# A hybrid attention layer: the attention gate's projection as seven half-size products, and the gated linear attention in steps of two chunks

## The chip, the core and the metric

The kernel runs on one core of a Trainium2 chip. The metric is the device time of one execution in microseconds (us), as the median of several. A core has TensorE (PE, matrix products; its weight loads are PEld), VectorE (DVE), ScalarE (ACT) and GpSimd (POOL), and SyncE (SP), which here issues every DMA. Matrix results go to PSUM, in banks of 512 float32 columns; everything else is in SBUF or in DRAM.

## What is computed

A layer on 1024 tokens (`x`) and 256 context tokens, width 1024. Both are normalised and modulated, and one projection `w_in` gives all streams:

```python
p = h @ w_in          # gq gk gv gg(gate) g_lr | dq dk dv dg(gate) | m_gla m_diff
...
s_f = gla_final_state(kc, vc, la_fc)          # from the context, per direction
o_gla = bidir_gla(q, k, v, la_f, la_b, s_f, s_b)
...
a = merge_heads(rms_norm(o_gla) * gla_gain) * jax.nn.silu(gla_gate)
b = merge_heads(rms_norm(o_diff) * diff_gain * (1 - lam_init)) * jax.nn.silu(diff_gate)
y = jax.nn.sigmoid(m_gla) * (a @ w_br_gla) + jax.nn.sigmoid(m_diff) * (b @ w_br_diff)
return y @ w_out
```

GLA (gated linear attention) has 4 heads with keys of 128 and values of 256 columns. It goes over the tokens in chunks; inside a chunk there are scores `q exp(cum) . k exp(-cum)` under a triangle, and between chunks a state of 128 x 256 that decays and takes in `k^T v`, once forward and once backward. Differential attention has 8 heads, two softmaxes each, with queries and keys normalised and rotated. Its gate `diff_gate` is `dg`, 1024 columns for the 1024 tokens.

## The kernel before

**Precision.** A projection is done in a fast float32 form: each operand is split into a high and a low part, and a product is three matmuls (`mm3`: high-high, high-low, low-high). A split is one ACT copy and one DVE subtraction (`split`). GLA's own products are plain float32, which the profile shows as two records a matmul.

**The order of the work is planned.** The kernel is written as generator tasks, and `Driver` runs them against a small model of engine costs when the program is built; so the order of instructions on PE, ACT, DVE and POOL is fixed by the tasks' priorities (a lower number goes first) and by what that model takes to be ready. `acq(tag)` and `rel(tag)` take and give back buffers of a kind (`TAGS` has the counts); a task that finds none waits. Every operation is issued from one of a few lines: matmuls at L335 (`mm`), transposes at L361 (`tr`), the vector engines at L197 (`emit`), DMAs at L300 (`dma`). So the profile's groups are told apart by their tiles.

**The stages.**
1. `prologue` (to about 110 us): constants, modulation, normalisation, the transposed activations `h`.
2. `stream` in `phase_a` (L857) runs projections as 512-column jobs, one after another at priority 9: `jobs` are gk, gq, and the first half of the GLA gate (`gg[0]`). Beside them `job_lr` and `job_la` make the decays, and `sums` (L886) makes four sums of blocks of `h`, stored as `d_s`. `wstream` loads weights through three `raw` buffers of 512 KB and splits them into `w` (18 tiles: nine blocks).
3. `pairs` (L987) does the value projections `gv` and `dv` by seven products of half-size blocks in place of eight (p1 to p7, with sums of blocks on both sides): two groups `g` of 1024 columns, five row tiles (four of the latent tokens for each half of the rows, one of the context). `pair_weights` (L918) loads the weight blocks and makes their sums. A group's accumulators lie in `mm` (3 banks), `gs`, `go`; the second ones in `tp`, `tp`, `gt`. `copy`, `add`, `out` and `direct` take results out. The blocks of `d_s` come back as `z` in `g5`. With the second group `job_gate` (L745) is started, after all weight blocks are loaded (`ev_pl`): it makes the output gate's vector from `w_ada` on DVE, through `raw`, and stores it as `d_gb`.
4. `to_gla` (L1142) waits for the decays, for `d_gb` and for the pairs' buffers, and starts four `gla_head`s. The late projections go on beside them: `dk[0], gg[1], dk[1], dg[0], dq[0], m, dq[1], dg[1]`; `dg` is a plain job of eight tiles for each 512 columns, with `post_gate` (L1340: tanh on ACT, a product on DVE, a product with `gdif` on POOL, store `d_dg`).
5. When GLA (`ev_b2`) and the late projections (`ev_stream`) are both done, attention starts (`to_b`), with the rest of the projections (`fill`) as filler; then the output (`phase_c`).

**A GLA head** (L1358), 10 chunks of 128 tokens, two of them context; a group `g` is two chunks. `prep` loads keys and decays and scans them on DVE; odd heads use the space `hk` of the context's `h`, which comes free when the last context tile of `dk[1]` is done. `kstates(e)` (L1431), per direction and group: exponential on ACT, product with k on POOL, two transposes, copy to `gkt`, before it goes on to the next group. `backward` runs through the chunks from the last and keeps the states `gsb`; each update (`upd`, L1469) is one matmul into `gt` and one DVE operation. `intra` (L1540), per group: the query factors `gqe` of both directions (ACT, POOL), the score factors (`factors`, L1504: differences, exponentials, products into `gkk` and `gqr`; a POOL memset makes the zero block), then for each chunk eight records of score matmuls into `gs`, a copy, two triangles on POOL (`affine_select`), a sum on DVE (`gsc`); only then the next group. `forward` (L1603), per chunk: three matmuls into `go` (forward state, backward state, scores), then `post` (L1639: square, root, product with the gate's rows, two transposes, split, store `d_aT`), then the forward update.

Of the kernel before, what the change touches and what calls it, by code (L numbers as in the profile page):

```python
# [11 lines left out]
F32R = mybir.dt.float32r  # L12
# [216 lines left out]
class Hybrid:  # L229
# [10 lines left out]
        gk=("sbA2", 1), gla=("sbA2", 2), gq=("sbA2", 1), gsb=("sbA2", 8), gsf=("sbA2", 2), ge=("sbA2", 2),  # L240
        gkt0=("sbA2", 2), gkt1=("sbA2", 2), gqe=("sbA2", 4), gqr=("sbA2", 2), gd=("sbA2", 2), gx=("sbA2", 2),
        gkk=("sbA2", 2), gsc=("sbA2", 2), gp=("sbA2", 4), gpl=("sbA2", 2), gv0=("sbA2", 2), gv1=("sbA2", 2),
# [502 lines left out]
    def job_gate(self):  # L745


        yield self.ev_pl
# [63 lines left out]
    def phase_a(self):  # L812
# [8 lines left out]
        self.gla_done, self.gla_free, self.gla_back, self.gla_intra = ([Event() for _ in range(4)] for _ in range(4))  # L821
# [17 lines left out]
        dg = nat(C_DG, (x8, x8), lambda c, i, pm: self.post_gate(1, c, i, pm))  # L839
        jobs = [tra(C_GK, [0, 1, 2], self.post_gk), tra(C_GQ, [0, 1], self.post_gq), gg[0]]  # L840
        late = [dk[0], gg[1], dk[1], dg[0], dq[0], dq[1], dg[1]]
# [11 lines left out]
        wp = self.pair_weights((C_GV, C_DV), wd.loaded[-1], last)  # L853
# [20 lines left out]
        d.spawn(self.consts_late(), At(105.0), prio=2)  # L874
        d.spawn(self.sums(), prio=3)
# [7 lines left out]

    SUMS = ("s2", "s1", "s3", "s4")

# [32 lines left out]
    def pair_weights(self, cols, ev_load, ev_run):  # L918
# [3 lines left out]
        wp = {(g, n, k): Event() for g in range(2) for n in RIGHT for k in range(4)}  # L922
# [4 lines left out]
        ev_l = {(g, n, kk): Event() for g in range(2) for n, kk, _ in LOADS}  # L927
# [13 lines left out]
        def run():  # L941
            yield ev_run
            for g in range(2):
# [43 lines left out]
    def pairs(self, wp):  # L987
# [3 lines left out]
        def loads():  # L991

            for g in range(2):
# [4 lines left out]
            for g in range(2):  # L998
                for n in self.SUMS:
                    for k in range(4):  # L1000
                        yield self.ev_s[n, k]
                        yield from self.acq("g5")
                        z = self.t("g5", [P, 2, 640], F32R)
                        self.dma(z, self.d_s[n, k])
# [16 lines left out]
        def mms(g, n, k, t, pm, first, last):  # L1021
# [5 lines left out]
            if t == 4:  # L1027
# [6 lines left out]
        for g in range(2):  # L1034
            if g:
                d.spawn(self.job_gate(), prio=2)
# [4 lines left out]
            def out(g, r, c, t, x, tag):  # L1041

                o = self.tok(8 + r if t == 4 else 4 * r + t)
                if g == 0:
# [41 lines left out]
            for t in range(5):  # L1086
# [7 lines left out]
            for n, ev, dst, nxt, tag in (("p6", "x", U, "u", "x2"), ("p5", "u", U5, "u5", "p")):  # L1094
                for k in range(4):
                    for t in range(5):
# [5 lines left out]
            for t in (0, 1, -1, 2, -2, 3, -3, 4, -4, -5):  # L1102
# [9 lines left out]
            for k in range(4):  # L1112
                for t in range(5):
# [6 lines left out]
    def direct(self, g, t, pm, tag):  # L1120

        o = self.tok(8 if t == 4 else t)
        if g == 0:
# [18 lines left out]
    def to_gla(self):  # L1142
# [8 lines left out]
        self.pool.memset(self.fresh.rearrange("p (c t) -> p c t", t=P + 1)[:, :, 0], 0.0)  # L1151
        for h in range(4):
            self.gla_head(h)
# [1269 lines left out]
```

## Time and profile before

| what | us |
|---|---|
| time, median of 3 runs | 1690.53 (1687.66 to 1690.86) |
| the profiled execution's own time | 1693.12 |
| its span, from the first to the last instruction | 1691.4 |
| TensorE busy | 1649.2 |
| VectorE busy | 1140.7 |
| ScalarE busy | 781.4 |
| GpSimd busy | 617.6 |
| pairs, about | 209 to 399 |
| GLA, from the store of `d_gb` to the last store of `d_aT` | 422 to 827 |
| first score matmul of attention | 910.6 |

Times inside a profile count from the span's start. In a row of the profile `mm<-w,h` means that an instruction writes tile `mm` and reads `w` and `h`; `x12` is the number of instructions; "idle before" and "releaser" say how long the engine stood and what it waited for. A matmul's own duration contains the pipeline behind it, so the price of one in a row of them is the distance from start to start.

### The profile page before, as it was taken

Reading aid. Unit: us, or ns where it says so; the run is one execution under the profiler, and the core shown is the slowest. Engines: PE = TensorE matmul, PEld = TensorE weight load, DVE = VectorE, ACT = ScalarE, POOL = GpSimd, SP = SyncE. Lnnn points to the kernel's source line nnn. Section 1 sums busy time; section 2 is a strip of 40 time slices with the busy share of each in tenths; the row PEclk is TensorE's granted clock in tenths of the full one; section 3 lists DMA queues with packets and bytes.
Section 4 is the critical chain, followed back from the end, with each engine's and each line's share of the span. In section 5 each row is a group of like instructions: output and inputs, shape, how many; then the busy total and the mean of one; then the engine's idle time right before and its main releaser. Section 6 shows DMA issues by size and latency. Waiting matters only on the chain.

```text
span 1691.4 us, 24621 instructions
## 1 busy us (share of the span) xinstructions
PE 1649.2 (98%) x8437; PEld 1366.0 (81%) x8437; DVE 1140.7 (67%) x2027; ACT 781.4 (46%) x1632; POOL 617.6 (37%) x743
## 2 busy tenths in 40 slices
PE   7999999999999999999999999999999899999999
PEld 3788888888888888888887788888887787887887
DVE  4787743466856866775553988777787787526694
ACT  4766522343444445455232666655656555411231
POOL 1500300002554655553342555455665455700000
PEclk9999999999999999999999999999999999999999
DMA  8556847588737466453851444436368451279431
GB/s 306 172 202 235 303 159 266 178 280 284 224 119 222 134 177 197 131 177 108 245 163 53 106 116 122 129 91 162 104 172 251 140 164 60 91 234 340 151 100 75
DMA packets 259950, 293.43 MB, mean 173 GB/s; under 512 B 21961, under 2 KB 182641, under 8 KB 259825
## 3 DMA queue, kind: packets, MB, share of 16 engines
q1 hardware_dynamic: 259824, 291.85, 55.0%
q8 instruction: 67, 1.10, 0.3%
q14 instruction: 59, 0.48, 0.1%
HBM read 194.27 MB, written 97.52 MB: 173 GB/s over the span
## 4 chain that ended last, share of the span: by engine, by line
PE 82%; DVE 7%; DMA 5%; ACT 2%; issue 2%; POOL 2%; SPq 0%; DVEq 0%; ACTq 0%; POOLq 0%
PE mm L335 33%; PE mc L335 10%; PE mb L335 7%; PE s L335 6%; PE b L335 5%; PE go L335 4%; PE b L361 3%; PE tp L335 3%; PE gt L335 3%; DVE sm L197 3%; PE gs L335 3%; PE tp L361 2%; POOL at L197 2%; DVE e L197 1%; ACT e L197 1%
## 5 line engine op out<-in xcount | busy, mean ns | idle before, releaser
L335 PE MATMUL mm<-w,h 128*128 128x512 f32 x1608 | 401.6, 400 | 0.0
L335 PEld LDWEIGHTS mm<-w,h 128*128 128x128 f32 x1608 | 297.4, 188 | 60.1 <-issue 0.5
L197 DVE TENSOR_REDUCE sm<-s 128x1 f32<-128x1024 f32 (+1 forms) x192 | 194.5, 1038 | 23.9 <-PE s L335 22.0
L335 PE MATMUL mb<-h,wt 128*128 128x512 f32 x744 | 205.1, 408 | 2.5 <-ACT ft L197 2.1
L197 ACT ACTIVATE e<-s,sm 128x1280 f32<-128x1280 f32 x128 | 170.1, 1331 | 69.2 <-DVE sm L197 61.5
L197 POOL TENSOR_TENSOR at<-ac,at 128x512 fp32r<-128x512 f32 x128 | 185.1, 1446 | 10.7
L335 PE MATMUL s<-hk,aq 128*128 128x512 f32 (+1 forms) x768 | 180.7, 369 | 4.1 <-issue 1.5
L197 POOL TENSOR_SCALAR at<-ac 128x512 fp32r<-128x512 f32 x128 | 100.7, 787 | 202.2 <-ACT ac L197 182.6
L335 PEld LDWEIGHTS mb<-h,wt 128*128 128x128 f32 x744 | 131.1, 190 | 25.9 <-ACT ft L197 3.6
L335 PEld LDWEIGHTS s<-hk,aq 128*128 128x128 f32 x768 | 124.3, 193 | 24.9 <-ACT e L197 4.9
L335 PE MATMUL mm<-h,w 128*128 128x512 f32 x576 | 142.4, 398 | 1.4 <-DVE h L197 1.0
L335 PE MATMUL mc<-h,wt 128*128 128x512 f32 x600 | 140.8, 392 | 1.4 <-DVE wt L197 0.5
L197 POOL TENSOR_TENSOR sm<-sm,nhalf 128x1 f32<-128x1 f32 (+2 forms) x110 | 113.8, 1035 | 56.4 <-DVE sm L197 49.6
L335 PEld LDWEIGHTS mc<-h,wt 128*128 128x128 f32 x600 | 111.4, 188 | 26.1 <-DMA h<-d_bT 2.4
L335 PE MATMUL b<-at,vv 128*128 128x256 f32 x960 | 131.9, 287 | 0.5 <-POOL at L197 0.4
L335 PEld LDWEIGHTS b<-at,vv 128*128 128x128 f32 x960 | 124.1, 192 | 5.7 <-POOL at L197 1.2
L335 PEld LDWEIGHTS mm<-h,w 128*128 128x128 f32 x576 | 106.1, 188 | 23.6 <-DVE h L197 1.5
L197 ACT ACTIVATE p<-mm 128x512 f32<-128x512 f32 (+1 forms) x111 | 64.1, 587 | 130.0 <-PE mm L335 112.0
L197 ACT ACTIVATE ac<-b 128x512 f32<-128x512 f32 x120 | 71.3, 601 | 89.6 <-PE b L361 84.4
L197 DVE SCALAR_TENSOR_TENSOR e<-e,sm,e 128x1280 f32<-128x1280 f32 x64 | 108.7, 1699 | 0.6
L197 DVE TENSOR_TENSOR w<-raw,w 128x512 fp32r<-128x512 f32 x120 | 88.0, 751 | 29.1 <-ACT w L197 24.2
L361 PE MATMUL b<-ident,e 128*128 128x128 f32 x598 | 93.3, 277 | 14.2 <-DVE b1k L197 4.8
(282 smaller groups left out, 2697.4 us busy)
## 6 DMA issues: line engine op xcount, KB each, us to landing
raw<-in_w_in SPq DMA_DIRECT2D x66, 512.0 KB, 4.7
g<-d_s SPq DMA_DIRECT2D x32, 640.0 KB, 5.3
aq<-d_qT SPq DMA_DIRECT2D x128, 128.0 KB, 3.1
d_dv<-pl SPq DMA_DIRECT2D x40, 256.0 KB, 5.3
d_kT<-pl SPq DMA_DIRECT2D x40, 256.0 KB, 2.9
gv<-d_v SPq DMA_DIRECT2D x40, 256.0 KB, 3.2
hk<-d_kT SPq DMA_DIRECT2D x32, 320.0 KB, 5.2
vv<-d_dv SPq DMA_DIRECT2D x16, 640.0 KB, 5.9
```

The lines of the kernel that those rows point to most:

```text
L197: self.ins = f(out, *args, **kw).ins
L335: self.ins = self.nc.tensor.matmul(out, lhsT, rhs, start=start, stop=stop, skip_group_check=more).ins
L361: self.nc.tensor.transpose(out, src, self.ident[:n, :n])
```

## The change

It does five things. **(1)** The gate `dg` leaves the late projections and becomes the third group of `pairs`, with four row tiles, as it has no context (`nt = 4`). `out` gains its tanh, product and POOL product; `direct` uses `post_gate`. **(2)** `job_gate` starts at 110 us on the planner's clock, without waiting for `ev_pl`. **(3)** The late projections are `dk[0], dk[1], gg[1], dq[0], dq[1], m`. **(4)** GLA goes in steps of two chunks: two updates' products in one `gt` bank, six outputs in one `go` bank, scores of two chunks in one `gs` bank, four transposes in one `tp` bank, one square, root, copy, triangle and store for two chunks. **(5)** GLA's tasks are taken apart: `kstates` hands the transposes to `turned`; `intra` makes factors only and hands scores to `pairs`; the query factors are a task `inter`; the forward states are a task `fstates`; `forward` has only outputs. `gkk` becomes one tile for each direction, zeroed once, and differences and exponentials are made in place in it.

```diff
-        late = [dk[0], gg[1], dk[1], dg[0], dq[0], dq[1], dg[1]]
+        late = [dk[0], dk[1], gg[1], dq[0], dq[1]]
...
+        d.spawn(self.job_gate(), At(110.0), prio=2)
...
+    BY7 = (("gv", C_GV), ("dv", C_DV), ("dg", C_DG))
...
-        for g in range(2):
-            if g:
-                d.spawn(self.job_gate(), prio=2)
+        for g, (what, _) in enumerate(self.BY7):
+            nt = 4 if what == "dg" else 5
...
+                if self.BY7[g][0] == "dg":
+                    yield from self.acq("p")
+                    th = self.t("p", [P, 512])
+                    yield d.on("ACT", x)
+                    yield On(self.act.activation(th, x, AF.Tanh, scale=0.5), "DVE")
+                    e = self.dve.scalar_tensor_tensor(x, th, 1.0, x, ALU.add, ALU.mult)
+                    self.rel("p", e)
+                    yield e
+                    xv = x.rearrange("p (n w) -> p n w", w=P)
+                    self.pool.tensor_tensor(xv, xv, self.gdif.unsqueeze(1).to_broadcast([P, 4, P]), ALU.mult)
...
-            for t in (0, 1, -1, 2, -2, 3, -3, 4, -4, -5):
+            for t in (0, 1, -1, 2, -2, 3, -3, 4, -4, -5) if nt == 5 else (0, 1, -1, 2, -2, 3, -3, -4):
...
-                yield AtPE(self.pool.tensor_tensor(ex, st["k"][:, sl], ex, ALU.mult))
...
+                en = self.pool.tensor_tensor(ex, st["k"][:, sl], ex, ALU.mult)
+                d.spawn(turned(e, g, ex, kt, v), AtPE(en), prio=2)
...
+        def products(e, g, js):
+
+            kt, v = st[e, g]
+            yield from self.acq("gt")
+            pu = self.t("gt", [P, 2, 256])
+            for j in js:
+                en = self.mm(pu[:, j], kt[:, j], v[:, j], True, True)
+            yield en
+            return pu
...
+            for g in range(1, 5):
                 qr, kr, ev = [None] * 2, [None] * 2, E(2)
                 for e in range(2):
                     d.spawn(factors(e, g, qr, kr, ev[e]), prio=3)
                 for e in range(2):
                     yield ev[e]
...
+                d.spawn(pairs(g, qr, kr), d.whenpe(*qr, *kr), prio=2)
...
+        def forward():
...
+                yield ev_sc[g]
+                yield ev_qe[g]
+                yield ev_sb[2 * g]
+                yield ev_sf[2 * g + 1]
...
+                po = self.t("go", [P, 2, 256])
                 for j in range(2):
                     c = 2 * g + j
+                    self.mm(po[:, j], qe[0][:, j], st["sf", c], True, False)
+                    self.mm(po[:, j], qe[1][:, j], st["sb", c], False, False)
+                    en = self.mm(po[:, j], sc[:, j, 0], v[:, j], False, True)
...
         d.spawn(prep(), prio=1)
         d.spawn(kstates(1), prio=2)
         d.spawn(bwd(), prio=1 if h else 0)
+        d.spawn(fstates(), prio=0)
         d.spawn(forward(), prio=0)
```

More of the change, by code (lines that the diff above doesn't have):

```diff
@@ L942, in run @@
             yield ev_run
-            for g in range(2):
+            for g in range(len(cols)):
                 def blk(n, k):
@@ L997, in loads @@
             yield self.ev_la
-            for g in range(2):
+            for g, (what, _) in enumerate(self.BY7):
+                w = 512 if what == "dg" else 640
                 for n in self.SUMS:
```

318 lines of the change are left out of this document (168 added, 150 removed).

## Prediction

> **What bounds the kernel now.** I read the page's first lines, then the busy times by stage, then the waits of TensorE in the stage that changes, then the chain.
>
> ```profile
> span 1691.4 us, 24621 instructions
> PE 1649.2 (98%) x8437; PEld 1366.0 (81%) x8437; DVE 1140.7 (67%) x2027; ACT 781.4 (46%) x1632; POOL 617.6 (37%) x743
> PE 82%; DVE 7%; DMA 5%; ACT 2%; issue 2%; POOL 2%; SPq 0%; DVEq 0%; ACTq 0%; POOLq 0%
> ```
>
> ```profile
> core 0: us, PE busy (x) PEld busy (x) DVE busy (x) ACT busy (x) POOL busy (x), PEclk, DMA share, GB/s
> 110.00:209.00 99.00, 99.00 (x462) 82.79 (x461) 78.69 (x104) 62.29 (x90) 12.08 (x8) 1.00 0.71 254
> 209.00:399.00 190.00, 189.12 (x833) 155.94 (x832) 94.07 (x145) 63.61 (x109) 1.82 (x2) 1.00 0.66 232
> 422.00:827.00 405.00, 403.56 (x2034) 338.54 (x2033) 273.55 (x536) 190.95 (x536) 212.39 (x346) 1.00 0.58 170
> 827.00:911.00 84.00, 82.50 (x379) 67.91 (x378) 38.05 (x61) 19.88 (x32) 33.09 (x30) 1.00 0.51 146
> ```
>
> TensorE works 98% of the span and carries 82% of the chain. The stages above are, in order: the first projections; the pairs (value columns by seven products); GLA beside the late projections; the late projections alone. TensorE is full in all four, at granted clock 1.00. In GLA's 405 us, DVE is busy 68%, POOL 52%, ACT 47%: none is near its limit on average, and what TensorE lost to waits there and up to 911 is this little:
>
> ```profile
> PE s L335 <- issue: 1.5, 1, 1.5
> PE tp L361 <- DVE gp L197: 0.7, 1, 0.7
> PE gt L361 <- DVE gsf L197: 0.4, 1, 0.4
> PE go L335 <- DVE gsc L197: 0.2, 1, 0.2
> ```
>
> So GLA's latency is hidden now: the projections (priority 9) fill every gap. A GLA that overlaps better has at most 1.3 us of waits (0.7+0.4+0.2) to give back. What counts is **how many TensorE instructions** remain, and whether new waits appear.
>
> **The change, part by part.**
>
> ```profile
> 208.84 2.72 PE tp L335 x12
> ...
> 875.03 34.08 PE mm L335 x150
> 910.60 2.56 PE s L335 x12
> ```
>
> *1. The gate by seven products.* The chain gives the price of a 512-column projection matmul: 12 in 2.72 us among the pairs, 150 in 34.08 us at the end of the late projections (the gate's own second column block), both 0.227 us. Removed: 2 blocks x 8 tiles x 8 k x 3 = 384. Added: 7 products x 4 k x 4 tiles x 3 = 336. So 48 fewer, 48 x 0.227 = **-10.9 us**, on the path, as TensorE is full where they go and where they come. The new group lasts 336 x 0.227 = 76.3 us.
>
> Beside it new work appears: 28 weight splits, 20 sums of weight blocks, 12 additions, 16 gate products on DVE.
>
> ```profile
> L197 DVE TENSOR_TENSOR w<-raw,w x120: 660/685/1711, 24.6 to 863.7; 128x512 fp32r<-128x512 f32 x120
> L197 ACT ACTIVATE p<-mm x111: 384/598/612, 60.8 to 909.2; 128x512 f32<-128x512 f32 x107, 128x256 f32<-128x256 f32 x4
> ```
>
> ```profile
> raw<-in_w_in SPq DMA_DIRECT2D x66, 512.0 KB, 4.7
> g<-d_s SPq DMA_DIRECT2D x32, 640.0 KB, 5.3
> aq<-d_qT SPq DMA_DIRECT2D x128, 128.0 KB, 3.1
> ```
>
> At 0.69 us that is 76 x 0.69 = 52 us of DVE in 76 us: TensorE hides it, as in the two groups before (94 of 190 us). DMA (size and median landing in the rows): 16 sums at 512 of 640 columns (8.4 MB) and ten weight blocks (5.2 MB) in 76 us are 180 GB/s, with 4 MB of stores 233, against 232 measured in the pairs. One margin shrinks. With four tiles instead of five, a product comes back to tile 0 after 9 matmuls (2.04 us) instead of 12 (2.72); in between ACT must copy that tile out (0.60 us) and two semaphores pass. A weight of t2 must be ready every 2.72 us instead of 3.4, through two sums and a split (three times 0.69 plus ACT 0.6). Cost between 0 (five tiles show no wait) and four tiles' copies and late weights, 4 us; I take **+1.5**.
>
> *2. The output gate's vector (job_gate) starts at 110 us instead of inside the pairs.* Its 16 DVE operations leave the pairs, and with them a wait of 0.9 us, behind which the chain shows a `gb` operation ahead of the weight splits.
>
> ```profile
> PE tp L335 <- DVE p L197: 0.9, 1, 0.9
> ...
> 377.27 0.04 DVE gb L197
> ```
>
> That is **-0.9**. They arrive where DVE is 79% busy (78.69 of 99), and its eight 0.5 MB loads take one of the three `raw` buffers at priority 2, ahead of the weight stream's 3.
>
> ```profile
> L197 DVE SCALAR_TENSOR_TENSOR gb<-raw,col,gb x14: 741/752/1417, 350.5 to 414.3; 128x512 f32<-128x512 f32 x14
> ...
> 114.02 1.59 SPq L300 DMA_DIRECT2D raw<-in_w_in  x2
> ...
> 120.58 0.63 ACT L197 ACTIVATE w<-raw 128x512 fp32r<-128x512 f32 x1 [0.23 <-DMA raw<-in_w_in]
> ```
>
> 16 x 0.75 = 12 us bring DVE to 91 of 99. Behind them in DVE's queue stand weight splits and the sums; behind a gate load in the queue of SP stand weight loads. The page of waits has none for TensorE between 110 and 209, but ACT at 120.58 split a weight the moment it landed: no slack at that switch of projections. If the gate takes the buffer freed at 114, the next weight load goes 1.2 us later and shares the DMA; two switches (about 115 and 160) are exposed. Bounds: 0, and 1.2 plus one load's landing, 4.7, about 6 us in all. I take **+2**.
>
> *3. GLA in pairs of chunks, tasks apart.* The same products: 18 state updates, 32 score matmuls, 24 output matmuls and 16 output transposes a head (each full-precision matmul shows as two records). What could change is the cost of breaking into the projections.
>
> ```profile
> 486.04 0.59 PE L335 MATMUL gt<-gv,gkt 128*128 128x256 f32 x2
> 486.28 1.74 PE L335 MATMUL mm<-w,h 128*128 128x512 f32 x6
> 487.86 0.59 PE L335 MATMUL go<-gsf,gqe 128*128 128x256 f32 x2
> 488.29 0.59 PE L335 MATMUL go<-gsb,gqe 128*128 128x256 f32 x2
> ```
>
> A lone update delays the projection by 0.24 us (486.04 to 486.28), and the six projection matmuls after it last 1.58 instead of 1.36: 0.46 in all. Inside a row the step is 0.43. So each of some 80 merges saves 0.03 by this pair, 2.4 us, or nothing. I take **0** (bounds -2.4 and +2.4). The vector engines do the same elements in fewer, longer instructions; the fixed zero block saves 32 POOL memsets. All this is under TensorE's cover.
>
> *4. Order.* GLA opens after three groups, and the late projections are dk, dk, gg1, dq, dq, m. The rotary table for dq is now loaded at dq's own start; its 0.5 MB and two POOL products take some 8 us, against three PSUM buffers of 5.4 us each: **0**, up to 2.
>
> Sum: -10.9 -0.9 +1.5 +2 = **-8.3 us**. Profiled span 1691.4 becomes 1683.1, that execution's 1693.12 becomes 1684.8; against the median 1690.53, which is 2.6 below the profiled execution, **1682.2**.
>
> **Does GLA still fit?** This is what could undo it.
>
> ```profile
> L300 SPq DMA_DIRECT2D d_gb<-gb x1: 333/333/333, 422.2 to 422.2; - x1
> L300 SPq DMA_DIRECT2D d_aT<-gpl x64: 359/386/925, 495.0 to 827.1; - x64
> L335 PE MATMUL mm<-w,hk x96: 387/392/586, 446.5 to 543.5; 128*128 128x512 f32 x96
> 543.19 0.39 ACT L197 ACTIVATE gp<-go 128x256 f32<-128x256 f32 x1 [0.91 <-PE go L335]
> 614.85 0.39 ACT L197 ACTIVATE gp<-go 128x256 f32<-128x256 f32 x1 [3.22 <-PE go L335]
> ...
> 694.55 0.38 ACT L197 ACTIVATE gp<-go 128x256 f32<-128x256 f32 x1
> ...
> 527.23 2.42 PE L335 MATMUL mm<-w,hk 128*128 128x512 f32 x9
> ```
>
> It opened at 422 (after the gate's store) and stored its last rows at 827: 405 us, with the stream's end at 910.6. After, the pairs end at 399+76 = 475, GLA opens near 485, the stream ends near 902: room 417. Even the old pace fits, barely. It gets shorter: between 543 and 615 no output was made, because head 1 needs `hk`, which the context tiles (mm<-w,hk, the last at 543.5) hold until 121 us after opening. With dk second in line these are tiles 9 to 12 of the late stream: 12 x 24 x 0.227 = 65 us after 475; with transposes and GLA's share of TensorE once it runs (an estimate of 30%: the 18 tiles before the context tiles hold 98 us of matmuls and took the 128 from 399 to 527) about 566, 81 us after opening. So GLA lasts about 365 even at the old pace: 50 us to spare. Heads 2 and 3 need gg1, whose first tile comes near 640, before head 2's outputs: before, these came 272 us after opening (the squares of `go` at 694.6), so at about 717, 40 earlier against the opening.
>
> **The rivals.**
>
> *A, slower: GLA becomes the bound.* The overlap makes DVE and POOL meet more often, and POOL slows.
>
> ```profile
> L197 POOL TENSOR_TENSOR ge<-hk,ge x20: 724/740/1696, 560.5 to 795.5; 128x256 f32<-128x256 f32 x20
> L197 POOL TENSOR_TENSOR gqe<-gq,gqe x32: 721/783/1187, 455.3 to 797.2; 128x256 f32<-128x256 f32 x32
> L197 POOL TENSOR_SCALAR_AFFINE_SELECT gsc<-gsc x64: 284/295/837, 467.2 to 809.1; 128x128 f32<-128x128 f32 x64
> L300 SPq DMA_DIRECT2D aq<-d_qT x128: 512/592/1778, 827.6 to 1408.9; - x128
> ```
>
> The same instruction takes up to 1.70 us where its median is 0.74. If all were as slow as the slowest: 40 x 0.96 + 32 x 0.40 + 32 x 0.54 = 68 us, all on GLA's chain: 365 + 68 = 433, 16 past the room. Then the queries' first four loads (4 x 0.59, plus 3.1 to land by the row above) start late, 5.5 more, and nothing else is left for TensorE: +21.5 - 8.3 = +13, **1704**. It decides from 50 us of lengthening. Against it: the medians sit at the minima, and three vector engines have a third of their time free. Chance 0.14. [...]
>
> *B, no change: the early gate and the tight pairs eat the gain.* Two weight switches with only two buffers, each a landing late (2 x 4.7), in place of +2: -10.9 -0.9 +1.5 +9.4 = -0.9, **1689.6**. For it: the missing slack at 120.58. Against it: only the third and fourth load of a switch are exposed. Chance 0.16.
>
> *C, faster still: breaking in costs more than the pair of rows shows.* If each of 80 merges saves a whole 0.22 us (the excess of the six matmuls), -17.6 more: **1664.6**. Against it: the 0.43 step inside a row. Chance 0.06.
>
> *D, it doesn't do what it says.* The overlap shortens GLA and the time doesn't follow, as TensorE is full anyway: that is inside the forecast.
>
> **How the numbers follow.** Forecast 0.64: with all bounds at their best -10.9 -0.9 -2.4 -1.3 = -15.5, 1675; at its worst up to the edge of "same". Differences of 0.2%, 3.4 us, are about what a measurement of this kernel can tell from none: below 1687.1 is faster, above 1693.9 slower. Faster: 0.64 + 0.06 = 0.70; same 0.16; slower 0.14. The range 1675 to 1694 takes in the forecast and B; A and C, 0.20, are left out.
>
> **What would show it.** Right: 7 x 48 matmuls in about 76 us after 399; the first score matmul near 902 instead of 910.6; the last d_aT store well before, at 830 to 870; TensorE's waits up to then under 6 us. Step 2 wrong: waits for `w` or a weight load between 115 and 170. Step 1 wrong: waits for `x2` or `w` between 420 and 435. A: the last d_aT store after 900 and a hole before the first score matmul. C: runs of projection matmuls nearer to 0.227 each beside GLA.

## The result and the profile after

The changed kernel takes 1695.59 us (median of 15 runs, 1692.97 to 1702.45) against 1689.16 of the kernel before (15 runs, 1686.71 to 1693.02): a ratio of 1.0039 with a 95% interval of 1.0031 to 1.0047. It is **slower by 6.4 us**, 0.4%; the forecast was 1682.2, 0.5% faster, in a range from 1675 to 1694. (The 1690.53 of the kernel before that the forecast starts from is the median of the first three of its 15 runs.) A ratio given with its interval is the record's own, not that of the two medians. Figures by stage come from one profiled execution of each kernel.

First the page of the changed kernel: its span, its busy times and the chain by engine.

```profile
span 1696.0 us, 24386 instructions
...
PE 1644.3 (97%) x8389; PEld 1360.1 (80%) x8389; DVE 1169.1 (69%) x2035; ACT 788.9 (47%) x1624; POOL 601.3 (35%) x649
...
PE 42%; DVE 6%; DMA 2%; ACT 2%; issue 2%; POOL 1%; SPq 0%; DVEq 0%; ACTq 0%; POOLq 0%
```

The 48 matmuls are gone (8389 records against 8437). The share of TensorE in the chain cannot be set against the earlier 82%: here the inferred chain accounts for about 55% of the span in all. The busy times by stage say more: the opening, the three groups of pairs, GLA beside the projections, the projections alone.

```profile
core 0: us, PE busy (x) PEld busy (x) DVE busy (x) ACT busy (x) POOL busy (x), PEclk, DMA share, GB/s
110.00:217.00 107.00, 103.56 (x468) 84.24 (x468) 90.35 (x123) 63.20 (x90) 14.75 (x10) 0.98 0.79 274
217.00:484.00 267.00, 265.35 (x1164) 217.59 (x1163) 138.60 (x206) 94.40 (x165) 18.65 (x13) 1.00 0.66 230
487.00:853.00 366.00, 357.50 (x1824) 301.21 (x1823) 277.40 (x515) 174.49 (x483) 204.30 (x263) 0.99 0.58 173
853.00:919.00 66.00, 65.26 (x298) 53.67 (x297) 22.72 (x36) 16.05 (x26) 14.69 (x14) 1.00 0.56 159
```

Two things are new. TensorE stood 3.4 us in the opening (107.00 less 103.56), where it stood not at all, and 8.5 us in GLA's stage (366.00 less 357.50), where it stood 1.4; and in both the granted clock is below 1.00. The other engines are a little fuller in GLA's stage than before, but far from full: DVE 76% (68% before), GpSimd 56% (52%), ScalarE 48% (47%). Three single waits make 8.4 of these 11.9 us. Here is TensorE's own timeline around each, the wait in square brackets:

```profile
196.84 1.82 PE L335 MATMUL tp<-gb,ones 128*128 128x512 f32 x2 [2.51 <-DVE gb L197]
197.67 4.69 PE L335 MATMUL mm<-w,h 128*128 128x512 f32 x12
```

```profile
655.71 0.94 PE L335 MATMUL mm<-w,h 128*128 128x512 f32 x3
660.05 1.12 PE L361 MATMUL tp<-ident,p 128*128 128x128 f32 x4 [3.40 <-POOL p L197]
660.82 1.63 PE L335 MATMUL mm<-w,h 128*128 128x512 f32 x3
```

```profile
817.28 0.94 PE L335 MATMUL mm<-w,h 128*128 128x512 f32 x3
820.73 0.66 PE L361 MATMUL tp<-ident,p 128*128 128x128 f32 x4 [2.50 <-POOL p L197]
```

Each time a small instruction (a matmul with the ones, or four transposes of one tile) stands ahead of projection matmuls in TensorE's queue and waits for a vector engine. The rows show TensorE taking its queue in order: the projections start only after it. How much they could have done meanwhile differs. After 196.84 a long row of them follows without another wait. At 660 DVE splits the next weights from 656.7 to 657.6 and from 658.4 to 659.1, during the wait, so the projections could have filled a part of it. At 820 hardly any: DVE, too, is behind, and splits their weights only after the wait.

```profile
821.14 1.28 DVE L197 TENSOR_TENSOR w<-raw,w 128x512 fp32r<-128x512 f32 x2
821.88 2.50 PE L335 MATMUL mm<-w,h 128*128 128x512 f32 x5 [0.26 <-DVE w L197]
```

And each wait is followed by something else, which the windows of 2 us around the second one show (the column after POOL's is the granted clock):

```profile
656.00:658.00 2.00, 0.66 (x3) 0.19 (x1) 1.98 (x4) 1.11 (x3) 2.00 (x4) 0.99 0.66 153
658.00:660.00 2.00, 0.00 (x0) 0.00 (x0) 1.98 (x3) 0.00 (x0) 2.00 (x2) 0.50 1.22 313
660.00:662.00 2.00, 1.95 (x7) 1.75 (x8) 0.44 (x2) 0.60 (x1) 1.83 (x2) 0.50 0.52 194
662.00:664.00 2.00, 2.00 (x7) 1.54 (x6) 2.00 (x3) 0.00 (x0) 1.93 (x3) 0.50 0.61 177
664.00:666.00 2.00, 2.00 (x9) 1.71 (x8) 0.21 (x1) 0.00 (x0) 0.00 (x0) 0.81 0.31 90
```

After 3.4 us of standing, TensorE runs at half clock until about 665: 2 us times (0.50 + 0.50 + 0.19) = 2.4 us of work lost while it was busy again. So a wait of 3.4 us cost 5.8.

Adding up such windows from one milestone to the next gives a ledger, in which "idle" is the window less TensorE's busy time, "slow clock" is the window times one less the granted clock (a part of it can fall on idle time), and the pairs start with the first second-product matmul:

| stage | before | after | forecast of the step |
|---|---|---|---|
| start of the pairs | 208.7 | 217.2 (+8.5) | +2 |
| pairs, to their last product | 189.0 | 266.8 (+77.8) | +76.3 +1.5 -0.9 = +76.9 |
| from there to the first score matmul | 512.9 | 434.8 (-78.1) | -87.2 |
| of this idle / slow clock | 3.0 / 0.0 | 9.2 / 5.1 | |
| first score matmul | 910.6 | 918.8 | 902 |

After the first score matmul the two executions differ by -3.6 us (1691.4 - 910.6 against 1696.0 - 918.8). That part lasts 773 to 783 us in the profiles of both kernels and of the eighteen below, with nothing there changed in kind, so I read nothing into it. It also means that one profile cannot show a gain of a few us in the whole time; the medians have to.

### The profile page after: what moved, and what is told of

It is laid out like the page before. It is cut to its first block, busy times and chain, and to the rows that moved or that the text cites. A ratio compares the mean times of both kernels' runs of the same rounds, so it can differ in the third digit from the quotient of the medians.

```text
span 1696.0 us, 24386 instructions
## 1 busy us (share of the span) xinstructions
PE 1644.3 (97%) x8389; PEld 1360.1 (80%) x8389; DVE 1169.1 (69%) x2035; ACT 788.9 (47%) x1624; POOL 601.3 (35%) x649
## 4 chain that ended last, share of the span: by engine, by line
PE 42%; DVE 6%; DMA 2%; ACT 2%; issue 2%; POOL 1%; SPq 0%; DVEq 0%; ACTq 0%; POOLq 0%
PE mc L335 10%; PE mm L335 7%; PE mb L335 7%; PE s L335 6%; PE b L335 5%; DVE sm L197 4%; PE b L361 3%; DVE e L197 2%; POOL at L197 1%; ACT e L197 1%; DMA h<-d_bT 1%; PE mz L335 1%; PE go L335 1%; PE tp L361 1%; DMA b1k<-d_dg 0%
## 5 line engine op out<-in xcount | busy, mean ns | idle before, releaser
L335 PE MATMUL mm<-w,h 128*128 128x512 f32 x1260 | 321.4, 404 | 0.9 <-DVE w L197 0.6
L335 PEld LDWEIGHTS mm<-w,h 128*128 128x128 f32 x1260 | 233.3, 190 | 48.9 <-DVE w L197 1.4
L335 PE MATMUL mm<-h,w 128*128 128x512 f32 x576 | 136.7, 394 | 3.1 <-ACT p L197 1.5
L197 POOL TENSOR_TENSOR sm<-sm,nhalf 128x2 f32<-128x2 f32 (+2 forms) x94 | 108.0, 1149 | 53.8 <-DVE sm L197 48.3
L197 ACT ACTIVATE w<-raw 128x512 fp32r<-128x512 f32 x120 | 72.5, 629 | 74.5 <-DVE raw L197 22.8
```

What stands on the lines that cost most here:

```text
L197: self.ins = f(out, *args, **kw).ins
L335: self.ins = self.nc.tensor.matmul(out, lhsT, rhs, start=start, stop=stop, skip_group_check=more).ins
```

## The experiments

**The theory** from these profiles: the instructions were priced rightly, and the loss is these waits of small instructions in TensorE's in-order queue, with the slow clock behind them. The rivals: all of it is the early gate; or GLA's new tasks make the waits; or the plan, drawn anew, would make such waits whatever was changed. ("The early gate" is `job_gate` at 110 us.) Medians are against the kernel before, run beside it on the same chip (1688.7 to 1690.4). The changed kernel was not run again beside them, so differences from its 1695.59 can be off by such 2 us.

### Parts alone

e1 gives the kernel before the early gate only; e2 the third group only (the output gate's vector at its old place, so after the third group's weights); e3 the new GLA only.

```diff
 e1
-        yield self.ev_pl
+        d.spawn(self.job_gate(), At(110.0), prio=2)
...
-            if g:
-                d.spawn(self.job_gate(), prio=2)
 e2   (BY7, nt and the dg branches as in the change; old GLA)
+        late = [dk[0], gg[1], dk[1], dq[0], dq[1]]
+            if g == 1:
+                d.spawn(self.job_gate(), prio=2)
 e3   (the change's gla_head; dg, late and job_gate as before)
```

> The kernel before with one part of the change: the output gate's vector starts at 110 us. Theory (three waits: TensorE's in-order queue holds a small instruction whose operand a vector engine has not finished, at 196, 660 and 820 us of the changed kernel, and TensorE's granted clock is low for some us after each; 3.7, 5.8 and 4.4 us): the wait at the gate's ones matmul comes back, the pairs start 6 to 9 us later than 208.7, the time is 4 to 8 us over the kernel before. Rival (the prediction's step 2: weights late by +2, old wait of 0.9 gone): +1. Rival (all the loss is in GLA's stage): 0.

> The kernel before with one part of the change: the attention gate as a third group of seven products; the old GLA, the output gate's vector with the second group as before, the late projections in the old order without the gate's two jobs. Theory (three waits): 48 matmuls less and no new long wait, -9 us, about 1680. Rival (the shorter late stage leaves GLA's tasks too little cover, so the waits come from it): TensorE waits of 2 us and more before the first score matmul, and less than 4 us gained.

> The changed kernel's GLA (steps of two chunks, tasks apart) alone: two groups of pairs, the attention gate as plain jobs, the old order and the old place of the output gate's vector. Theory (three waits; GLA's tasks fill the queues of ScalarE and GpSimd so that the planned order stands before a tile that is late): one or two waits of 2 us and more at transposes of p between 520 and 850, +5 to +12 us over the kernel before. Rival (the prediction's step 3): within 2 us. Rival (the new order or the third group makes the waits): within 2 us too, and no wait at p.

Measured: e1 1700.69 (1.0062, 1.0046 to 1.0078), e2 1701.53 (1.0066, 1.0049 to 1.0083), e3 1697.64 (1.0041, 1.0027 to 1.0055). Each part alone is slower by 7 to 11 us, 29 in sum, and together they cost 6.4: the parts are not additive. e1 bears the theory out at the start (pairs at 216.6, the wait for `gb` again 2.50) and adds 4.6 us in a GLA stage in which no instruction was changed. e3 loses 7.5 idle and 3.4 slow clock in GLA's stage, in several waits of 1.0 to 1.4, none of them over 2: more than the prediction's 0, but not the one long wait I expected.

e2 was a miss, in an instructive way. TensorE's timeline at the end of its GLA stage:

```profile
914.14 0.41 PE L361 MATMUL tp<-ident,gp 128*128 128x128 f32 x2 [1.65 <-DVE gp L197]
...
917.92 0.41 PE L361 MATMUL tp<-ident,gp 128*128 128x128 f32 x2 [2.08 <-DVE gp L197]
923.46 2.90 PE L335 MATMUL s<-hk,aq 128*128 128x512 f32 x8 [5.12 <-DMA aq<-d_qT]
```

The projections are used up and TensorE waits for GLA's last outputs, then 5.12 us for the first queries. This is the prediction's rival A in its outcome, GLA as the bound, though not by slower vector engines. Its `d_gb` was stored at 521.0 and its last `d_aT` at 919.2: with the gate's vector behind three groups of weights, the old GLA opens late and lasts 398 us.

### The old place of the gate's vector, and the order

e4 is the changed kernel with `job_gate` at its old place; e8 is e2 with the changed kernel's order of the late projections.

```diff
 e4
-        d.spawn(self.job_gate(), At(110.0), prio=2)
+        yield self.ev_pl
+            if g == 1:
+                d.spawn(self.job_gate(), prio=2)
 e8   (e2 with)
+        late = [dk[0], dk[1], gg[1], dq[0], dq[1]]
```

> The changed kernel with the output gate's vector back at its old place (with the second group, after all weight blocks are loaded, here those of three groups). Theory (three waits): the wait at 196 is gone, the pairs start near 209, 6 to 8 us less than the changed kernel, near 1688, and the waits at p in GLA's stage stay. Rival (the prediction's step 2): -1. Rival (the two waits in GLA's stage hang on what came ahead and go too): near 1682.

> As the run of the gate by seven products with the old GLA, but with the changed kernel's order of the late projections (second block of dk second). There GLA ended last: transposes of gp waited at 914 and 918, then the first score matmul 5.1 us for its queries. Theory (the context's space comes free 50 us earlier and GLA fits): last store of d_aT before 895, no such waits, first score matmul near 905, 10 us less than that run. Rival (the old GLA is too slow in any order, so the change's two-chunk GLA is what lets the gate's gain through): waits at gp after 900 again, within 4 us of that run.

Measured: e4 **1684.25** (0.9977, 0.9955 to 0.9998), e8 1699.58 (1.0056, 1.0039 to 1.0073). In e8 the first score matmul waits 5.56 us for its queries again; `d_gb` at 517.6, last `d_aT` at 914.8: 397 us. So the order does not shorten the old GLA when it opens late, and the rival holds: with the late opening, only the two-chunk GLA (e4: 519.0 to 892.1, 373 us) ends before the projections do. Here are e4's opening, its pairs and its GLA.

```profile
110.00:209.00 99.00, 99.00 (x466) 82.94 (x465) 78.74 (x107) 62.55 (x90) 11.18 (x7) 1.00 0.71 254
209.00:482.00 273.00, 268.54 (x1168) 219.62 (x1167) 145.34 (x215) 94.47 (x165) 20.87 (x15) 0.99 0.65 229
520.00:893.00 373.00, 370.51 (x1902) 313.06 (x1901) 278.69 (x519) 182.30 (x496) 204.47 (x259) 1.00 0.61 180
```

The opening has no idle time, GLA's stage 2.5 us (373.00 less 370.51) at clock 1.00. What it pays is 4.5 us in the pairs, where the gate's sums now stand among the third group's: a wait of 2.97 us at 466 and the slow clock after it (1.7 us in e9's expectation below; mean clock 0.99 in the row of the pairs). That e4 also mends GLA's stage was the rival's result, not mine.

### Is it the plan?

e6 and e7 change no instruction: the planner is told that GLA's tasks start 1 us later, in the kernel before (e6) and in the changed one (e7). e12 does the same to e4.

```diff
+        yield AtPE(self.d.now + 1.0)
         for h in range(4):
             self.gla_head(h)
```

> The kernel before, with the planner told to start GLA's tasks 1 us later: the same instructions, another order of them on the engines from there on. Theory (the order planned for GLA's stage is what loses time: a small TensorE instruction stands before an operand that is late on the chip, and any new plan draws new waits): idle and slow-clock time of TensorE between the pairs and the first score matmul moves by 3 us or more from the 3.0 of the kernel before, time +2 to +10. Rival (the waits belong to the change's own parts): within 2 us.

> The changed kernel with the same 1 us told to the planner. Theory (new plan, new waits): the two waits at 660 and 820 are not the same ones; idle plus slow clock in GLA's stage moves by 4 us or more from 14.3, to either side; the wait at 196 stays. Rival (the waits belong to the change's own parts): the waits at transposes of p stay, 14 within 2.

> The changed kernel with the output gate's vector at its old place (1684.25, 3.2 of idle and no slow clock in GLA's stage), with GLA's tasks planned 1 us later. Theory (that low loss is one draw of the planned order): idle plus slow clock in GLA's stage rises to 6 to 14, time +3 to +10. Rival (without the early gate GLA's stage is planned well): within 2 us of 1684.25.

Measured: e6 1692.79 (1.0017, 1.0006 to 1.0027), e7 1688.97 (0.9992, 0.9977 to 1.0006), e12 1685.75 (0.9981, 0.9972 to 0.9991). For the changed kernel the theory holds: with the same instructions, the waits at 660 and 820 are gone, idle plus slow clock in GLA's stage falls from 14.3 to 7.3, and the median is 6.6 us lower, as much as the whole measured loss. (2.4 us of it can lie in the opening, where the order is the same in both: the pairs start at 214.8 instead of 217.2, as no slow clock followed the wait for `gb`.) The two longest groups of TensorE's waits in that stage of e7:

```profile
PE go L335 <- DVE gp L197: 2.5, 1, 2.5
PE tp L361 <- POOL p L197: 1.2, 1, 1.2
```

One of 2.5 is left, at another operand. For the kernel before the shift adds 1.8 us of such loss (4.8 against 3.0), less than expected, and for e4 next to nothing (3.5 against 3.2): there the theory of a mere draw is wrong. Something in e4 keeps the loss low.

### Where the opening's loss comes from

In ten kernels without gate work ahead of the pairs (before, e2, e3, e4, e6, e8, e12, and e9, e11, e14 below) the pairs start at 208.7 to 211.4, 209.9 on average; in five with all of it (after, e1, e7, and e10, e13 below) at 214.8 to 218.1, 216.6 on average. The difference, 6.7 us, is the price of the early gate. e5 moves the ones matmul behind the pairs; e15 and e16 keep its loads or its sums alone, and so leave out most of the gate's vector; e17 gives the loads a buffer of their own.

```diff
 e5
                 self.rel("raw", e)
+        yield self.ev_pd            # set after the pairs
+        for n in range(2):
+            o = 2048 + n * 512
             yield from self.acq("p")
 e15  (e5 with 8 of 512 columns in 14 of 16 sums)
 e16  (e5 with 8 of 512 columns loaded)
 e17  (e5 with)
-                yield from self.acq("raw")
+                yield from self.acq("x4")
```

> The changed kernel; the output gate's vector still starts at 110 us, but its last step (bias load, ones matmul, bias sum) waits until the pairs are done. Theory (the early gate costs by the ones matmul that stands in TensorE's queue for a late DVE sum, and by the slow clock after it): no wait at 196, pairs start at 209 to 212, the stage from 110 to there shows under 1 us of idle TensorE and no clock loss; time 4 to 12 us under the changed kernel, as GLA's stage is planned anew too and may lose anything from 3 to 14 us there. Rival (the gate's loads and DVE sums ahead of the weight splits cost it): pairs start at 215 or later without that matmul.

> The changed kernel with the ones matmul after the pairs (pairs started at 214.1 in that run, 209 to 211 without the early gate), and of the gate's sums 14 of 16 cut to 8 of 512 columns, the loads kept; it leaves out most of the output gate's vector, so y is not the reference's. Theory (loads take the weight stream's buffers and bandwidth): pairs start at 213 to 215 still. Rival (the sums stand ahead of the weight splits on VectorE): 209 to 211.

> The counterpart: all 16 sums at full width on VectorE, but each of the eight loads cut from 512 KB to 8 KB (one column is used for all), which leaves out most of the output gate's vector, so y is not the reference's. Theory (loads take the weight stream's buffers and bandwidth): pairs start at 209 to 211. Rival (the sums stand ahead of the weight splits on VectorE): 213 to 215.

> The changed kernel; the gate's eight loads go through the one x4 buffer, which is idle until the pairs' weights, instead of the three raw buffers of the weight stream, and the ones matmul comes after the pairs. All loads and sums are made, from about 110 us on. Theory (the held raw buffers delay the weight stream): pairs start at 209 to 212, no wait for w over 1 us between 110 and there; against the run with the ones matmul after the pairs (214.1, 1689.8) 3 to 5 us less, 1685 to 1688. Rival (any early sums or loads delay the weight splits): 214 or later, 1690.

Measured: e5 1689.82 (1.0000, 0.9991 to 1.0010), pairs at 214.1; e15 1695.93 (1.0032, 1.0019 to 1.0045), pairs at 220.1; e16 1694.09 (1.0021, 1.0006 to 1.0037), pairs at 220.5; e17 1687.99 (0.9987, 0.9976 to 0.9999), pairs at 211.7. How the 6.7 us divide is less clear than these steps look. After, e1, e7, e10 and e13 have the same opening, instruction by instruction, and still start the pairs at 214.8 to 218.1; e5's 214.1 is 2.5 under their average and lies between its theory (209 to 212) and its rival (215 or later). TensorE still stands 3.2 us in e5's opening (3.4 in the changed kernel), now in waits for `w`, the longest 1.20 at 171: the plan was drawn anew, and other waits took the place of the one at `gb`. e17 starts 2.4 earlier than e5, by one profile each, with one wait for `w` of 1.6 us; that the held raw buffers cost this much is likely, not shown. e15 and e16 were meant to part loads from sums and did not: either alone costs at least as much as both. In e16 the loads are 1/64 of their size, and still ScalarE waits, in its own timeline:

```profile
168.14 0.74 ACT L197 ACTIVATE x<-g 128x640 fp32r<-128x640 f32 x1 [4.10 <-DVE g L197]
```

The sums on DVE delay a block sum `g`; ScalarE's copy of it waits 4.10 us for it, and behind that copy stands the weight split for which TensorE then stands 4.05 us at 172.57. So it is again an order, on two queues. The bytes alone are not the cause (e16 loads 1/64 of them), nor DVE's time alone (e15 cuts most of it); both still hold the raw buffers.

### GLA's opening, and repairs

In the kernels with three groups and the new GLA, the loss in GLA's stage goes roughly with the time from the end of the pairs to GLA's first scan (e14 below is left out: it opens at 164 us and GLA ends last). It is no rule: e3, with two groups and the new GLA, opens at 35 us and loses 10.9.

| first scan after the pairs | kernels | idle + slow clock |
|---|---|---|
| 12 us | after, e7, e10 | 14.3, 7.3, 11.3 |
| 24 to 26 us | e5, e9, e15, e16, e17; e11 | 6.9, 6.9, 5.2, 6.9, 5.2; 11.3 |
| 40 to 53 us | e13, e18, e4, e12 | 5.2, 5.8, 3.2, 3.5 |

e13 keeps the early gate and holds GLA back by 32 us; e18 is e17 with that. e10 plans the transposes of dk and dq tiles 4 us later.

```diff
 e13
     def to_gla(self):
+        yield AtPE(self.d.now + 32.0)
 e10  (post_qk)
-        yield AtPE(e)
+        yield AtPE(e + 4.0)
```

> The changed kernel, early gate and all, but GLA's tasks are held back by 32 us on the planner's clock, so that they open near 520 instead of 487. Theory (the opening is the cause: early GLA tasks stand between the dk tiles' own vector work, and the two kernels that opened at 519 to 521 lost 3.2 and 3.5 us in GLA's stage): idle plus slow clock of that stage 5 or less in place of 14.3, time 5 to 9 us under the changed kernel, with the start of the pairs still at 215 to 218. Rival (the plan is drawn anew and the loss is any from 3 to 14): 7 or more. Rival (GLA ends too late): last store of d_aT after 905 and a wait of 3 us or more at the first score matmul.

> The same, and GLA opens 32 us later on the planner's clock. Theory (raw buffers, and the early opening): pairs start at 209 to 212, pairs 267, idle plus slow clock in GLA's stage 3 to 6 in place of 14.3: 1680 to 1685, the fastest. Rival (GLA's end becomes late): last store of d_aT after 900 and a wait at the first score matmul, above 1688.

> The changed kernel; the four transposes of each dk and dq tile are planned 4 us later than the product that they read is due. Theory (these transposes stand in TensorE's queue before a GpSimd product that the chip finishes later than planned): no wait of TensorE at p from GpSimd over 1 us, idle plus slow clock in GLA's stage from 14.3 to 8 or less, time 5 to 8 us under the changed kernel; the wait at 196 stays. Rival (any new plan does as much, as the shift by 1 us did; waits at ge, gkk and gp take their place): idle plus slow clock 7 to 14 with other operands named.

Measured: e13 1690.43 (0.9996, 0.9984 to 1.0008), 5.2 us under the changed kernel, with the start of the pairs still at 216.5 and the last `d_aT` at 869.0. That fits the opening as a cause, but e13 is also a new plan, and e7's new plan gained 6.6 with the opening where it was; one run does not part the two. e18 1687.80 (0.9994, 0.9984 to 1.0004): the opening adds nothing to the own buffer, and at 212.1, 267.0 and 5.8 each stage is as expected, but the median is only 0.2 us below e17's, no difference. e10 1693.94 (1.0034, 1.0020 to 1.0049): no wait at `p` is left in GLA's stage, and 11.3 us of loss is. Its two longest groups of waits there:

```profile
PE mm L335 <- DVE w L197: 4.2, 3, 2.6
PE mm L335 <- ACT w L197: 1.9, 1, 1.9
```

The weights took the place of the transposes. Mending a wait at one operand does not mend the plan.

Two more places for the gate's vector made it slower, against what was expected: e9 (beside the second group of pairs, not waiting for `ev_pl`; e11 is e9 with e10's edit) and e14 (after the pairs).

```diff
 e9
-        d.spawn(self.job_gate(), At(110.0), prio=2)
...
+            if g == 1:
+                d.spawn(self.job_gate(), prio=2)      # without ev_pl; ones after the pairs
 e14
-        d.spawn(self.job_gate(), At(110.0), prio=2)
...
             yield from self.pairs(wp)
+            d.spawn(self.job_gate(), prio=2)
```

> The changed kernel with the output gate's vector summed on DVE beside the second group of pairs (without waiting for the weight blocks), its ones matmuls after the pairs. Theory (the early gate costs by its loads and sums ahead of weight splits, and the old place by sums in the tight third group: 3.0 of wait and 1.7 of slow clock at 463): pairs start 209 to 211, no wait over 1 us in the third group, GLA opens near 495; opening and pairs together 6 us less than the changed kernel's 374. GLA's stage, planned anew, may lose 3 to 14: 1678 to 1689. Rival (gate sums in the second group hit its weight sums as they did in the third): a wait of 2 us or more between 300 and 400.

> Both: the output gate's sums beside the second group and the transposes of dk and dq tiles planned 4 us later. Theory: opening and pairs as in the run with the sums beside the second group, GLA's stage with under 8 us of idle plus slow clock: 1678 to 1684, the fastest of these kernels. Rival (new waits in the place of the old): above 1686.

> The changed kernel with the output gate's vector made after the pairs, so nothing of it lies ahead of the pairs or in their third group. Theory: pairs start at 209 to 211, no wait of 2 us in the third group (the two kernels with the old place had 2.1 and 3.0 there), pairs 267 instead of 271 to 272; GLA opens at 510 to 520 and its stage loses 3 to 7; time 1679 to 1684, the fastest. Rival (the gate's loads delay the first weights of dk, as they delayed the weights in the second group by 40 us): a wait of 3 us or more for w or raw between 480 and 520, time above 1686. Rival (GLA ends too late): last store of d_aT after 905.

Measured: e9 1730.28 (1.0248, 1.0223 to 1.0272), e11 1729.72 (1.0237, 1.0217 to 1.0258), e14 1721.88 (1.0181, 1.0163 to 1.0199). In e9 the third group's weights stop; TensorE's timeline, then rows of the DMA issues on SP's queue in that time:

```profile
377.69 1.52 PE L335 MATMUL mm<-w,g 128*128 128x512 f32 x2 [40.66 <-ACT w L197]
```

```profile
328.84 0.38 SPq L300 DMA_DIRECT2D raw<-in_w_ada  x1
...
333.93 0.38 SPq L300 DMA_DIRECT2D raw<-in_w_ada  x1
...
339.63 27.11 SPq L300 DMA_DIRECT2D raw<-in_w_ada  x6
371.76 0.37 SPq L300 DMA_DIRECT2D raw<-in_w_in  x1
```

All eight loads of the gate go through the raw buffers before one more weight does. That is the prediction's rival B in the open: priority 2 ahead of 3 at the raw buffers. In e14 the weight stream holds the buffers instead, the gate's first load is issued at 530.4, `d_gb` comes at 630.9 and the last `d_aT` at 941.9: rival A.

No version is clearly faster than e4 and e12, which are 0.2% faster than the kernel before: about as little as these runs can tell from none.

## Why the prediction was wrong, step by step

**Step 1, the gate by seven products, was right within 2 us.** The third group took 79.4 us (from its first matmul at 405.3 to the late projections at 484.6) where 77.8 were priced (76.3 + 1.5), with waits for `w`, `p` and `pl` of 1.7 us in all. The two groups before it took 188.1 instead of 189.7, so the forecast -0.9 came true and a little more. At full clock and without idle time, the work from the end of the pairs to the first score matmul is about 420.5 us (434.8 - 9.2 - 5.1; some 1 us of the slow clock fell on idle time and is taken off twice), against 422.7 by the same count (512.9 - 3.0 - 87.2).

**Step 2, the early gate, failed in size and mechanism.** "I take **+2**" became +8.5 in the profiled execution, +6.7 on average over the kernels above. The step looked at weights behind loads and DVE sums; e5 and e17, which keep these and have no ones matmul there, start 4.2 and 1.8 us later than the average without the early gate. But its sign, waits for `w` between 115 and 170, came to only 1.0 us in the changed kernel. What it left out is that `job_gate` also issues a matmul, which stands in TensorE's queue for a DVE sum: a wait of 2.51 us and 1.7 of slow clock behind it. Taking it away brought other waits (e5), so the shares of the 6.7 stay open. The sum was itself late, as DVE's timeline shows, with GpSimd's row beside it.

```profile
192.89 0.81 DVE L197 TENSOR_TENSOR g<-g,g 128x640 f32<-128x640 f32 x1
193.78 1.60 DVE L197 SCALAR_TENSOR_TENSOR gb<-raw,col,gb 128x512 f32<-128x512 f32 x1
195.31 0.81 DVE L197 TENSOR_TENSOR g<-g 128x640 f32<-128x640 f32 x1
196.05 0.74 DVE L197 SCALAR_TENSOR_TENSOR gb<-raw,col,gb 128x512 f32<-128x512 f32 x1
```

```profile
192.24 2.60 POOL L197 TENSOR_TENSOR p<-p,ggla 128x512 f32<-128x512 f32 x1 [3.70 <-DVE p L197]
```

One sum took 1.60 us instead of 0.74, beside this GpSimd product of 2.60 us (1.73 and 1.79 for the ones before and after): the sum and the product each lasted some 0.8 us longer than their neighbours.

**Step 3, GLA's tasks, is where most was lost, and the failing sentence is "All this is under TensorE's cover".** The term was put at **0**; the stage came out at -78.1 where -87.2 was forecast, 9.1 us worse, with 14.3 us of idle time and slow clock against 3.0 before. At 660 and 820 the late instructions stood ahead of the projections in the queue, so these gave no cover: TensorE waited 3.40 and 2.50 us. The order is fixed by the planner's durations; where an operand was late, as there, cover turned into waiting. How the wait at 660 came about is in ScalarE's and GpSimd's timelines.

```profile
644.69 0.38 ACT L197 ACTIVATE gj<-go 128x256 bf16<-128x256 f32 x1 [3.13 <-PE go L335]
...
651.53 0.68 ACT L197 ACTIVATE ge<-hk,gbi 128x128 f32<-128x128 f32 x2
```

```profile
652.29 0.73 POOL L197 TENSOR_TENSOR ge<-hk,ge 128x256 f32<-128x256 f32 x1 [5.56 <-ACT ge L197]
653.39 1.29 POOL L197 TENSOR_TENSOR ge<-gk,ge 128x256 f32<-128x256 f32 x1 [0.37 <-ACT ge L197]
...
655.05 1.64 POOL L197 TENSOR_TENSOR sm<-sm,nhalf 128x8 f32<-128x8 f32 x1
656.64 1.21 POOL L197 TENSOR_SCALAR_AFFINE_SELECT gsc<-gsc 128x256 f32<-128x256 f32 x2
657.83 0.72 POOL L197 TENSOR_TENSOR gqe<-gq,gqe 128x256 f32<-128x256 f32 x1
658.51 1.49 POOL L197 TENSOR_TENSOR p<-p,sm 128x512 f32<-128x512 f32 x1
```

ScalarE's square of an output (still one for each chunk, 32 in all, not one for two chunks) waits 3.13 us for TensorE's output matmuls; behind it stand the factors' exponentials and, at 651.53, those of `ge`; GpSimd waits 5.56 us for these, then works almost without a break (7.17 of 7.76 us from 652.29 to 660.05), and the dk tile's product comes out at 660.0 behind them, for TensorE to wait on. Over the stage no vector engine is full; for these 8 us GpSimd and DVE (7.59 of 7.76 us) nearly are. The forecast bounded step 3 by what a merge costs on TensorE; it had no term for new waits, though it kept "TensorE's waits up to then under 6 us" as a sign: they came to 9.2 from the pairs' end on. That the plan makes these waits, and not the instructions alone, is what e7 shows.

**Step 4, the order: its sign was not tested alone in the changed kernel.** Its claim that the early context space shortens GLA found no support: with the old GLA opening late, e8 and e2 differ in the order and last 397 and 398 us. In the changed kernel GLA lasted 366 us (from its first load of keys at 487.3 to the last `d_aT`), which the prediction had as "about 365 even at the old pace"; the number was right by luck, as the shortening is the two-chunk GLA's (373 in e4).

**The rivals.** A did not happen in the changed kernel (last `d_aT` at 853.5, 65 us to spare), but is what e2, e8 and e14 ran into, at the price given for the queries (5.5; measured 5.1 and 5.6). GpSimd beside DVE, from which A starts, is in the trace of before: the four slowest single `ge` products (1.18 to 1.70 us, median 0.74) all ran beside DVE operations, though others beside DVE took 0.74. B was too narrow: its result, 1689.6, was nearer, by a mechanism that is only part of it. The case that came true, waits of TensorE in its own queue on both sides of the pairs, had no rival.

**What stays open.** Why one plan draws 14 us and another 7 with GLA opening at the same time is not settled, nor why e11 lost 11.3 where five kernels that open alike lost 5 to 7. That the loss falls with a later opening is a correlation, with e3 and e11 against it; e13 does not part it from a new plan. How the early gate's 6.7 us divide between the ones matmul, the buffers and the sums is open too. Whether a plan made with the measured durations would avoid these waits was not tried.

## What to carry to other kernels

In these runs a full TensorE did not hide what stood in its own queue ahead of the projections (waits of 2.51, 3.40 and 2.50 us in the changed kernel): price a change also by each small instruction that it puts into the busiest in-order queue, by who must finish before it, and by how late that one can be. Where an order is planned ahead from a model, change nothing but the plan as a control (here 1 us on the planner's clock moved the median by 6.6 us in one kernel, by 2.5 and 1.5 in two others) before a gain or loss is put down to an edit. And take parts out of a combined change one at a time as well as putting them in: here two parts, 11.3 and 7.4 us slower alone, made a slightly faster kernel together with the new order (e4).

## What the runs showed of the hardware that was not expected

The wait of 2.51 us before 196.84 in the changed kernel was followed by 1.7 us of lost clock:

```profile
194.00:196.00 2.00, 0.34 (x2) 0.00 (x0) 2.00 (x2) 0.00 (x0) 0.84 (x1) 1.00 0.49 196
196.00:198.00 2.00, 1.16 (x3) 0.63 (x3) 2.00 (x4) 0.45 (x1) 0.00 (x0) 0.79 0.98 296
198.00:200.00 2.00, 2.00 (x5) 1.26 (x4) 1.90 (x3) 2.00 (x4) 1.79 (x1) 0.50 0.99 269
200.00:202.00 2.00, 2.00 (x9) 1.56 (x9) 1.43 (x3) 0.17 (x1) 0.00 (x0) 0.86 1.02 378
```

The loss is 2 us times (0.21 + 0.50 + 0.14) = 1.7 us. In e7 the same matmul waited 2.50 us, and there was none:

```profile
194.00:196.00 2.00, 0.00 (x0) 0.00 (x0) 2.00 (x3) 0.00 (x0) 0.15 (x1) 1.00 0.56 170
196.00:198.00 2.00, 1.85 (x6) 1.24 (x7) 2.00 (x4) 1.13 (x2) 0.49 (x1) 1.00 0.91 324
198.00:200.00 2.00, 2.00 (x10) 1.63 (x9) 1.90 (x3) 1.49 (x3) 1.33 (x1) 1.00 0.84 284
```

In the changed kernel the granted clock stood at 0.50 for 3.4 us from 197.14, for 6.8 us from 657.94 and for 3.4 us from 821.78, which is a loss of 1.7, 3.4 and 1.7 us. These stretches did not start at one distance from the waits: the first 0.30 us after the wait's end at 196.84, the second 2.11 us before the end of the one at 660.05, the third 1.05 us after the end of the one at 820.73. Why the wait of 2.51 us was followed by a stretch at half clock, and e7's of 2.50 us at the same matmul was not, these runs do not show.
